# Softmax over rows of 32768: two column pieces of 8192 per tile, scaled by VectorE and ScalarE, with the small sums on GpSimd

## Chip, core, metric

One core of one Trainium2 chip. The metric is device time in microseconds of one execution. The span that a profile shows is about 2 us shorter than the time.

## The reference

```python
batch, seq, vocab = 16, 256, 32768          # float32 in, float32 out; temperature 1.0
scaled = logits / temperature
scaled = scaled - scaled.max(axis=-1, keepdims=True)
exp_scaled = np.exp(scaled)
return exp_scaled / exp_scaled.sum(axis=-1, keepdims=True)
```

These are 4096 rows. 536.87 MB must be read and as much written.

## The kernel before

A row is split in two halves, which lie in neighbouring partitions. A tile is 128 partitions x 16384 columns (64 rows, 8.39 MB), there are 64 tiles, and three buffers hold them in turn. Each full tile is loaded in two halves of 8192 columns. It is worked on in four pieces of 4096: VectorE takes the negated maximum of a piece, ScalarE does exp in place and sums. Then maxima and sums of the pieces and of the two half rows are combined by small instructions, and the pieces are scaled.

```python
_LOAD = (8192, 8192)
_PIECES = (4096, 4096, 4096, 4096)
_ON_DVE = (4096, 1024, 4096, 1024)      # columns of each piece scaled by VectorE, the rest by ScalarE
_HALF = 8192
...
for k in range(K):
    xc = xs[:, at[k] : at[k] + sizes[k]]
    nc.vector.tensor_reduce(out=nm[:, k : k + 1], in_=xc, axis=X, op=A.max, negate=True)
    ...
    nc.scalar.activation(out=xc, in_=xc, func=Exp, bias=nm[:, k : k + 1], scale=inv_t,
                         accum_out=ssum[:, k : k + 1])
nc.vector.tensor_reduce(out=nMh[:, 0:1], in_=nm, axis=X, op=A.min)
combine(nMh, A.min)                     # shuffle to the neighbour partition, then min
nc.scalar.activation(out=ee, in_=nm, func=Exp, bias=nMh[:, n_rounds : n_rounds + 1], scale=-1.0)
nc.vector.tensor_tensor_reduce(out=ttj, in0=ee, in1=ssum, ..., accum_out=Sh[:, 0:1])
combine(Sh, A.add)
nc.vector.reciprocal(out=rS, in_=Sh[:, n_rounds : n_rounds + 1])
nc.vector.tensor_scalar_mul(out=f, in0=ee, scalar1=rS)
for k in range(K):
    a, b, c = at[k], at[k] + on_dve[k], at[k] + sizes[k]
    if b > a:
        nc.vector.tensor_scalar_mul(out=xs[:, a:b], in0=xs[:, a:b], scalar1=f[:, k : k + 1])
    if c > b:
        nc.scalar.activation(out=xs[:, b:c], in_=xs[:, b:c], func=Copy, scale=f[:, k : k + 1])
    ...
    elif t and c % _HALF == 0:
        store(t, c - _HALF, c)          # issued from ScalarE's queue, the last two tiles' from SyncE
...
for t in range(G):
    normalise(t)
    if t and t + _BUFS - 1 < G:
        load(t + _BUFS - 1)             # issued from SyncE's queue
```

## Time and profile before

| | before |
|---|---|
| time, median (range) | 2493.26 us (2493.20 to 2493.26, 3 runs) |
| VectorE, ScalarE, GpSimd busy | 63%, 54%, 0% |
| DMA | 431 GB/s over the span |
| VectorE's instructions | 1217, 19 in a full tile |

The lines that carry the reading stand in the prediction below. In the DMA slices each digit is the busy share of a fortieth of the span in tenths. In a chain in order of time the columns are start, duration and what; in a group of instructions they are line, engine, operation, shapes, count, then busy us, mean ns, and idle us before with the engine that ended it. Two more lines of this kernel also belong here. The first is from the list of DMA queues (packets, MB, share of time), the second from the waits (us in total, times, longest):

```profile
q14 instruction: 22, 0.18, 0.0%
```

### The profile page before, as it was taken

What the parts mean: (1) busy time and instruction counts of PE and PEld (TensorE: products, weight loads), DVE (VectorE), ACT (ScalarE), POOL (GpSimd) and SP (SyncE); (2) the same over time, 40 slices, a digit from 0 to 9 for tenths busy, and PEclk for the clock granted to TensorE, in tenths of its full rate; (3) what the DMA queues carried; (4) which work ended last, traced back from release to release, by engine and by line L of the source; (5) the groups of instructions that cost most, each with busy time, mean ns of one, the idle gap of its engine ahead of it and who ended that gap; (6) DMA issues with size and microseconds to landing.
All of it is one profiled execution on the core that took longest, in us unless ns stands there. A gap on an engine that the chain in (4) does not pass through costs nothing.

```text
span 2491.5 us, 2807 instructions
## 1 busy us (share of the span) xinstructions
DVE 1580.1 (63%) x1217; ACT 1352.5 (54%) x711; POOL 0.2 (0%) x4
## 2 busy tenths in 40 slices
DVE  7765666655766657566675666756667566665654
ACT  6565555655556555555555554555545555465544
POOL 0000000000000000000000000000000000000000
DMA  9999999999999999999999999999999999999998
GB/s 412 436 430 436 431 435 431 433 433 430 437 430 437 430 436 430 437 429 436 431 436 431 434 432 432 434 431 436 430 437 429 437 430 436 430 437 430 436 431 370
DMA packets 38038, 1073.94 MB, mean 431 GB/s; under 512 B 4224, under 2 KB 4224, under 8 KB 4224
## 3 DMA queue, kind: packets, MB, share of 16 engines
q1 hardware_dynamic: 20160, 553.66, 51.6%
q10 hardware_dynamic: 17856, 520.10, 48.4%
q14 instruction: 22, 0.18, 0.0%
HBM read 536.87 MB, written 536.87 MB: 431 GB/s over the span
## 4 chain that ended last, share of the span: by engine, by line
DMA 68%; another core or an unknown queue 15%; DVE 11%; ACT 4%; issue 1%; SPq 0%; ACTq 0%
DMA out_dram<-x 41%; DMA x<-in_logits_dram 28%; DVE nm L108 8%; ACT x L115 3%; DVE x L148 3%; SPq L72 0%; DVE f L144 0%; ACT x L152 0%; ACT ee L129 0%; DVE rS L143 0%; DVE Sh L91 0%; DVE Sh L88 0%; DVE ttj L132 0%; ACTq L197 0%
## 5 line engine op out<-in xcount | busy, mean ns | idle before, releaser
L108 DVE TENSOR_REDUCE nm<-x 128x1 f32<-128x4096 f32 (+1 forms) x257 | 1119.1, 4395 | 639.0 <-DMA x<-in_logits_dram 639.0
L115 ACT ACTIVATE x<-x,nm 128x4096 f32<-128x4096 f32 (+1 forms) x257 | 949.3, 3694 | 976.4 <-DVE nm L108 976.0
L152 ACT ACTIVATE x<-x,f 128x3072 f32<-128x3072 f32 (+1 forms) x132 | 366.4, 2781 | 129.9 <-DVE f L144 73.5
L148 DVE TENSOR_SCALAR x<-x,f 128x1024 f32<-128x1024 f32 (+3 forms) x256 | 379.9, 1548 | 2.3
L132 DVE CUSTOM_DVE_ANT_0 ttj<-ee,ssum 128x4 f32<-128x4 f32 x64 | 10.4, 162 | 228.2 <-ACT ee L129 228.2
L115 ACT ACTIVATION_READ_ACCUMULATOR x<-x,nm 128x1 f32 x257 | 47.9, 186 | 0.0
L129 ACT ACTIVATE ee<-nm,nMh 128x4 f32<-128x4 f32 x64 | 18.0, 282 | 0.0
L144 DVE TENSOR_SCALAR f<-ee,rS 128x4 f32<-128x4 f32 x64 | 14.7, 229 | 2.2
L143 DVE RECIPROCAL rS<-Sh 128x1 f32<-128x1 f32 x64 | 10.5, 164 | 2.2
L91 DVE TENSOR_TENSOR Sh<-Sh 128x1 f32<-128x1 f32 x64 | 10.2, 159 | 2.2
L91 DVE TENSOR_TENSOR nMh<-nMh 128x1 f32<-128x1 f32 x64 | 10.2, 159 | 2.2
L127 DVE TENSOR_REDUCE nMh<-nm 128x1 f32<-128x4 f32 x64 | 10.0, 157 | 2.2
L88 DVE STREAM_SHUFFLE Sh<-Sh 128x1 f32<-128x1 f32 x64 | 9.7, 151 | 0.0
L88 DVE STREAM_SHUFFLE nMh<-nMh 128x1 f32<-128x1 f32 x64 | 9.7, 151 | 0.0
L115 ACT ACT_TABLE_LOAD x1 | 1.3, 1283 | 8.1 <-DMA x<-in_logits_dram 8.1
L132 DVE DVE_READ_ACCUMULATOR2_ANT Sh<- 128x1 f32 x64 | 5.2, 82 | 0.0
L88 DVE LOAD_MASK_SELECT nMh<-nMh x64 | 0.9, 14 | 2.8
L88 DVE LOAD_MASK_SELECT Sh<-Sh x64 | 0.9, 14 | 2.8
L183 POOL MEMSET const-bfloat16-1.0<- 128x1 bf16 x1 | 0.1, 101 | 0.0
L183 POOL MEMSET const-uint8-127<- 128x1 uint8 x1 | 0.1, 101 | 0.0
L183 POOL MEMSET const-float32-0.0<- 128x1 f32 x1 | 0.1, 98 | 0.2 <-issue 0.2
L183 POOL MEMSET const-float32-1.0<- 128x1 f32 x1 | 0.1, 98 | 0.0
## 6 DMA issues: line engine op xcount, KB each, us to landing
x<-in_logits_dram SPq DMA_DIRECT2D x124, 4096.0 KB, 31.3
out_dram<-x ACTq DMA_DIRECT2D x124, 4096.0 KB, 49.3
x<-in_logits_dram SPq DMA_DIRECT2D x7, 2048.0 KB, 20.6
out_dram<-x SPq DMA_DIRECT2D x2, 4096.0 KB, 33.5
out_dram<-x SPq DMA_DIRECT2D x3, 2048.0 KB, 17.3
x<-in_logits_dram SPq DMA_DIRECT2D x2, 1024.0 KB, 36.1
out_dram<-x SPq DMA_DIRECT2D x2, 1024.0 KB, 22.8
```

Of the source, the lines that this page charges most:

```text
L88: nc.vector.stream_shuffle(out=v[:, j + 1 : j + 2], in_=v[:, j : j + 1], mask=mask)
L91: nc.vector.tensor_tensor(out=v[:, j + 1 : j + 2], in0=v[:, j : j + 1], in1=v[:, j + 1 : j + 2], op=op,)
L108: nc.vector.tensor_reduce(out=nm[:, k : k + 1], in_=xc, axis=X, op=A.max, negate=True)
L115: nc.scalar.activation(out=xc, in_=xc, func=Exp, bias=nm[:, k : k + 1], scale=inv_t, accum_out=ssum[:, k : k + 1],)
L127: nc.vector.tensor_reduce(out=nMh[:, 0:1], in_=nm, axis=X, op=A.min)
L129: nc.scalar.activation(out=ee, in_=nm, func=Exp, bias=nMh[:, n_rounds : n_rounds + 1], scale=-1.0)
L132: nc.vector.tensor_tensor_reduce(out=ttj, in0=ee, in1=ssum, scale=1.0, scalar=0.0, op0=A.mult, op1=A.add, accum_out=Sh[:, 0:1],)
L143: nc.vector.reciprocal(out=rS, in_=Sh[:, n_rounds : n_rounds + 1])
L144: nc.vector.tensor_scalar_mul(out=f, in0=ee, scalar1=rS)
L148: nc.vector.tensor_scalar_mul(out=xs[:, a:b], in0=xs[:, a:b], scalar1=f[:, k : k + 1])
L152: nc.scalar.activation(out=xs[:, b:c], in_=xs[:, b:c], func=Copy, scale=f[:, k : k + 1])
L183: nc = _bacc.Bacc("TRN2", target_bir_lowering=False, num_devices=1)
```

## The change

The intent is fewer and larger instructions: two pieces of 8192, the first scaled by VectorE alone and the second by ScalarE alone, and the small sums off VectorE. The second tile keeps four pieces, so that the first tile's stores leave early; first and last tile are unchanged.

```diff
-_PIECES = (4096, 4096, 4096, 4096)
-_ON_DVE = (4096, 1024, 4096, 1024)
+_PIECES = (8192, 8192)
+_ON_DVE = (8192, 0)
+_SECOND_PIECES = (4096, 4096, 4096, 4096)
+_SECOND_ON_DVE = (4096, 4096, 2048, 0)
@@ combine takes the engine of its tensor_tensor
-    def combine(v, op) -> None:
+    def combine(v, op, engine=None) -> None:
+        engine = engine or nc.vector
...
+        if K == 2:
+            nc.gpsimd.tensor_tensor(out=ttj, in0=ee, in1=ssum, op=A.mult)
+            nc.gpsimd.tensor_tensor(
+                out=Sh[:, 0:1], in0=ttj[:, 0:1], in1=ttj[:, 1:2], op=A.add
+            )
+            combine(Sh, A.add, nc.gpsimd)
+            nc.vector.reciprocal(out=rS, in_=Sh[:, n_rounds : n_rounds + 1])
+            nc.gpsimd.tensor_scalar_mul(out=f, in0=ee, scalar1=rS)
+        else:
             ... (the sums on VectorE, as before)
@@ stores after all scaling
-            elif t and c % _HALF == 0:
-                store(t, c - _HALF, c)
+        for h in range(0, W if 0 < t < G - 1 else 0, _HALF):
+            store(t, h, h + _HALF)
```

More of the change, by code (lines that the diff above doesn't have):

```diff
@@ L48 @@
     n_rounds = _SPLIT.bit_length() - 1
-    K = max(len(_FIRST_PIECES), len(_PIECES), len(_LAST_PIECES))
+    K = max(
+        len(p) for p in (_FIRST_PIECES, _SECOND_PIECES, _PIECES, _LAST_PIECES)
+    )
     pool = ctx.enter_context(tc.tile_pool(name="fixed", bufs=1))
@@ L66, in cut @@
             return _LAST_PIECES, _LAST_ON_DVE, _LAST_PIECES
+        if t == 1:
+            return _SECOND_PIECES, _SECOND_ON_DVE, _LOAD
         return _PIECES, _ON_DVE, _LOAD
@@ L90, in combine @@
             )
-            nc.vector.tensor_tensor(
+            engine.tensor_tensor(
                 out=v[:, j + 1 : j + 2],
@@ L131, in normalise @@
         )
-        nc.vector.tensor_tensor_reduce(
-            out=ttj,
-            in0=ee,
-            in1=ssum,
-            scale=1.0,
-            scalar=0.0,
-            op0=A.mult,
-            op1=A.add,
-            accum_out=Sh[:, 0:1],
-        )
-        combine(Sh, A.add)
-        nc.vector.reciprocal(out=rS, in_=Sh[:, n_rounds : n_rounds + 1])
-        nc.vector.tensor_scalar_mul(out=f, in0=ee, scalar1=rS)
+        if K == 2:
+            nc.gpsimd.tensor_tensor(out=ttj, in0=ee, in1=ssum, op=A.mult)
+            nc.gpsimd.tensor_tensor(
+                out=Sh[:, 0:1], in0=ttj[:, 0:1], in1=ttj[:, 1:2], op=A.add
+            )
+            combine(Sh, A.add, nc.gpsimd)
+            nc.vector.reciprocal(out=rS, in_=Sh[:, n_rounds : n_rounds + 1])
+            nc.gpsimd.tensor_scalar_mul(out=f, in0=ee, scalar1=rS)
+        else:
+            nc.vector.tensor_tensor_reduce(
+                out=ttj,
+                in0=ee,
+                in1=ssum,
+                scale=1.0,
+                scalar=0.0,
+                op0=A.mult,
+                op1=A.add,
+                accum_out=Sh[:, 0:1],
+            )
+            combine(Sh, A.add)
+            nc.vector.reciprocal(out=rS, in_=Sh[:, n_rounds : n_rounds + 1])
+            nc.vector.tensor_scalar_mul(out=f, in0=ee, scalar1=rS)
         for k in range(K):
```

## The prediction

> **What bounds the kernel now.** I read the page from the top: busy shares, the slices of the span, the chain of waits; then the DMA queue's own waits, the issues, and one stretch in the middle in order of time.
>
> Busy shares and the DMA slices, from the page:
>
> ```profile
> DVE 1580.1 (63%) x1217; ACT 1352.5 (54%) x711; POOL 0.2 (0%) x4
> ...
> DMA  9999999999999999999999999999999999999998
> ...
> DMA packets 38038, 1073.94 MB, mean 431 GB/s; under 512 B 4224, under 2 KB 4224, under 8 KB 4224
> ```
>
> No compute engine is near full, while the DMA engines are at 90% or more in 39 of 40 slices and still moving in the last. The bytes are fixed: 536.87 MB in, 536.87 MB out.
>
> The chain of waits (page), and part of it in order of time:
>
> ```profile
> DMA 68%; another core or an unknown queue 15%; DVE 11%; ACT 4%; issue 1%; SPq 0%; ACTq 0%
> ```
>
> ```profile
> 1183.02 48.33 DMA out_dram<-x
> ...
> 1250.83 31.35 DMA x<-in_logits_dram
> ...
> 1282.20 8.76 DVE nm L108 x2
> ...
> 1299.15 48.32 DMA out_dram<-x
> ```
>
> The chain goes round one of three buffers: a store, a load, then compute. One turn is 1299.15 - 1183.02 = 116.13 us for three tiles, 38.71 us a tile. A tile moves 8.39 MB each way, so 16.78 MB / 38.71 us = 433.4 GB/s. The columns are start, duration and what; a transfer's duration includes waiting in its queue. That is the key to this page: 4.19 MB at 433.4 GB/s needs 9.68 us, yet a store is listed with 48. It stands behind other transfers.
>
> The timeline of that stretch (start, duration, engine, work):
>
> ```profile
> 1204.78 8.75 DVE L108 TENSOR_REDUCE nm<-x 128x1 f32<-128x4096 f32 x2 [10.26 <-DMA x<-in_logits_dram]
> ...
> 1217.27 0.28 ACT L129 ACTIVATE ee<-nm,nMh 128x4 f32<-128x4 f32 x1
> ...
> 1221.73 0.34 ACTq L81 DMA_DIRECT2D out_dram<-x  x1
> ...
> 1225.00 0.34 ACTq L81 DMA_DIRECT2D out_dram<-x  x1
> ...
> 1243.49 8.74 DVE L108 TENSOR_REDUCE nm<-x 128x1 f32<-128x4096 f32 x2 [10.26 <-DMA x<-in_logits_dram]
> ```
>
> Call T = 1204.76 the landing of a tile's second half. Its two stores are issued at T+17.0 and T+20.2. What still lies in the store queue then? The chain shows that the previous tile's first store, issued at 1183.02, lands at 1231.35, T+26.6; its second store lands one half-tile slot (38.71/2 = 19.36) later, T+45.9. So the store queue is not empty until T+45.9. The load queue has slack too: by the chain a store landed at 1231.35 and the next load went out at once, while the load ahead of it landed only at 1243.47, as the last row shows: 12 us of work was left. Hence the bound is DMA throughput; the tile's latency is hidden.
>
> **What the Trainium skill says.** "DMA: Bandwidth & Descriptors", section "Specifications", gives a fabric ceiling of 435 GB/s and an HBM limit near 358 GB/s per core. The trace agrees with the first (433.4) and goes past the second. At 435 GB/s the bytes alone take 2468 us, an estimate from that page; only 1% of the 2493 could go. The same page, section "Queues, rings and completion order", says each DMA engine goes round the queues that have work, packet by packet; so a later store costs nothing while both queues hold work. The trace agrees: a half-tile load takes a 19.36 us slot with stores beside it, twice 9.68. "GPSIMD Engine Reference", section "2.1 Instruction dispatch", describes software dispatch on eight cores and some 6 us for the first call of a freshly loaded routine. The trace of before has only four memsets of about 0.1 us on POOL and cannot confirm it.
>
> **The change part by part.** Durations by shape, from the groups by form:
>
> ```profile
> L108 DVE TENSOR_REDUCE nm<-x 128x1 f32<-128x4096 f32 x255 | 1114.7, 4412 | 639.0 <-DMA x<-in_logits_dram 639.0
> L115 ACT ACTIVATE x<-x,nm 128x4096 f32<-128x4096 f32 x255 | 945.3, 3707 | 976.4 <-DVE nm L108 976.0 <-ACT x L152 0.5
> L152 ACT ACTIVATE x<-x,f 128x3072 f32<-128x3072 f32 x124 | 354.0, 2856 | 127.6 <-DVE f L144 71.2 <-DVE x L148 34.1 <-DMA x<-in_logits_dram 22.4
> L148 DVE TENSOR_SCALAR x<-x,f 128x4096 f32<-128x4096 f32 x124 | 291.4, 2350 | 2.2
> L148 DVE TENSOR_SCALAR x<-x,f 128x1024 f32<-128x1024 f32 x124 | 92.7, 747 | 0.0
> ...
> L152 ACT ACTIVATE x<-x,f 128x1536 f32<-128x1536 f32 x7 | 10.5, 1564 | 2.3 <-DVE f L144 2.3
> ...
> L108 DVE TENSOR_REDUCE nm<-x 128x1 f32<-128x2048 f32 x2 | 4.5, 2275 | 0.0
> L115 ACT ACTIVATE x<-x,nm 128x2048 f32<-128x2048 f32 x2 | 4.0, 1986 | 0.0
> ```
>
> Two sizes of each operation give a line, and I extend it to 8192 columns. Reduce: 4412-2275 = 2137 ns per 2048, so 4412+2x2137 = 8.69 us. Exp: 1721 ns per 2048, 3707+2x1721 = 7.15 us. VectorE scale: (2350-747)/3072 = 0.522 ns a column, 2350+4096x0.522 = 4.49 us. ScalarE scale: (2856-1564)/1536 = 0.841, 2856+5120x0.841 = 7.16 us.
>
> VectorE, per full tile: reduces 4x4.41 to 2x8.69, -0.27; scaling 2x2.35+2x0.75 = 6.19 to 4.49, -1.70; the small product, its accumulator read, one add and f (0.162+0.082+0.159+0.229 on the page) go to GpSimd, -0.63. Sum -2.6; times the 61 tiles that take this path (all but the first, second and last of 64), about -159 us: busy 1580 to about 1421. ScalarE: exp 4x3.71 to 2x7.15, -0.53; two accumulator reads fewer at 0.186, -0.37; scaling 2x2.86 to 7.16, +1.45. Sum +0.55, +34 us: about 1386. GpSimd: four small operations a tile, 244 in all; I put each at 0.1 to 0.5 us, from memsets at 0.1 plus two inputs, an estimate. None of this busy time is on the bound.
>
> Latency after T: reduce 8.7, exp 7.15, ee 0.28 ends at about T+16.2 against T+12.8 before (T+3.4 later because the second exp starts after a whole half was reduced). Then the small sums: before from ee to f took about 1.1 us (ee ends 1217.55, scaling starts 1218.64). Now they cross VectorE and GpSimd five times; I take 2 us, at T+18.2. ScalarE's 7.16 ends at T+25.4. The rebuilt instruction order shows both store issues after that scaling, so they go out at T+25.4 and T+25.7, later by 8.4 and 5.5 us. The queue holds stores until T+45.9: 20 us to spare. So landings stay on their 19.36 us grid, the next loads go out at the same instants, and the next T is the same. What grows in compute shrinks as queueing: first-half stores show 48.3 - 8.4 = 40 us from issue to landing, second-half ones about 59. Sum on the path: 0.
>
> Ends: the first and last tile's code is unchanged. The second tile's first store is issued some 3 us later, behind the first tile's two stores. Near the end, the stores of tile 61 already wait for a load (the 22.4 us in the third row); the new order keeps such a wait, but now scaling comes before it. Tile 62 gives that back through larger pieces and should be stored within about 1 us of before, again with transfers queued ahead. I allow +-1 us.
>
> **The rivals.** (1) *Compute is on the chain, so its growth costs.* DVE 11% and ACT 4% stand in the chain, and 8.4 us times 61/3 turns would be +171 us: 2664. Against it: the queue wait in the same chain gives way first, 20 us worth. (2) *VectorE was the bound*, with 63% the busiest engine; -159 us would give 2334. Against it: VectorE waited 639 us for loads, and DMA is full. (3) *GpSimd is far slower than I think.* Small sums would have to take over 22 us a tile; each us beyond adds up to 61 us in all if the loads don't fill the gap. A first call of 6 us falls in the third tile alone and fits. (4) *Both stores issued together change the mixture on the DMA engines.* The four first quarter loads end at 4.9 us intervals, 2.10 MB each, 429 GB/s without stores: 1% below the mixed rate, so at most +20 us even if the mixture were lost, and it isn't, as both queues stay filled.
>
> **Range and chances.** The expected change is 0 with +-1 us from the ends and the odd hiccup, and three runs before agree within 0.1 us. I predict 2493.2 us, 2490.5 to 2496.5 in 8 of 10. Over 2% faster would need a DMA rate above 440 GB/s: 0.5%. Slower needs rival 1 or 3: 1.5%. Within 2%: 98%.
>
> **What would show it.** Right: DMA at 9s in every slice and near 431 GB/s; a turn of 116.1 us; loads' median still 31.3 us, stores' median fallen from 49.3 to between 40 and 59; VectorE near 1421, ScalarE near 1386. Wrong: slices of DMA under 9, a longer turn, a VectorE wait on GpSimd of many us, or first-half stores that take only about 20 us, which would mean the queue runs dry.

## More of the kernel before

```profile
DVE nm L108 <- DMA x<-in_logits_dram: 639.0, 73, 11.2
```

Queue 14 carries the engines' own instructions; 22 packets look like nothing. VectorE's wait of some 10 us per tile for a load is the slack of the computing engines.

## The result

| | before | after |
|---|---|---|
| median of 4 runs (range) | 2493.23 us (2493.11 to 2493.26) | 2490.66 us (2490.20 to 2491.36) |
| span of the profiled run | 2491.5 us | 2489.1 us |
| instructions in all; on VectorE | 2807; 1217 | 2138; 667 |

The ratio is 0.999, 95% interval 0.9973 to 1.0007. A ratio here is the mean time of one kernel's fast runs over that of the other's of the same rounds, so it is not quite the ratio of the medians. By that interval the two are the same; but the ranges don't touch, nor do they in any later comparison with the kernel before, so 2.6 us, a thousandth, is a difference worth explaining, if not worth having.

From the page of the changed kernel: busy times, the DMA slices, its packets, the instruction queue, the chain of waits, and the two largest groups of DMA issues.

```profile
DVE 1449.4 (58%) x667; ACT 1391.5 (56%) x406; POOL 53.5 (2%) x248
...
DMA  9999999999999999999999999999999999999999
...
DMA packets 38033, 1073.90 MB, mean 431 GB/s; under 512 B 4224, under 2 KB 4224, under 8 KB 4224
...
q14 instruction: 17, 0.14, 0.0%
...
DMA 62%; another core or an unknown queue 15%; DVE 13%; ACT 7%; POOL 1%; issue 1%; SPq 0%; ACTq 0%
...
x<-in_logits_dram SPq DMA_DIRECT2D x124, 4096.0 KB, 30.2
out_dram<-x ACTq DMA_DIRECT2D x124, 4096.0 KB, 45.2
```

The DMA engines are as full as before. The share of compute in the chain rose from 15% to 21% and nothing was lost by it. Part of the chain in order of time:

```profile
1186.99 44.36 DMA out_dram<-x
...
1250.75 30.05 DMA x<-in_logits_dram
...
1303.10 44.50 DMA out_dram<-x
```

A buffer's turn is 1303.10 - 1186.99 = 116.11 us, against 116.13 before. Inside it the store gave up 4 us, from 48.3 to 44.4. The timeline of the same stretch (start, duration, engine, work, idle time and who ended it):

```profile
1203.43 8.69 DVE L115 TENSOR_REDUCE nm<-x 128x1 f32<-128x8192 f32 x1 [7.88 <-DMA x<-in_logits_dram]
...
1219.27 0.28 ACT L136 ACTIVATE ee<-nm,nMh 128x2 f32<-128x2 f32 x1
...
1221.18 7.12 ACT L169 ACTIVATE x<-x,f 128x8192 f32<-128x8192 f32 x1 [1.64 <-POOL f L147]
1221.18 4.49 DVE L165 TENSOR_SCALAR x<-x,f 128x8192 f32<-128x8192 f32 x1 [0.42 <-POOL f L147]
1225.59 8.68 DVE L115 TENSOR_REDUCE nm<-x 128x1 f32<-128x8192 f32 x1
1225.71 2.97 ACTq L87 DMA_DIRECT2D out_dram<-x  x2
```

Three things are to be seen. The sums take 1221.18 - 1219.55 = 1.6 us. The first store goes out at 1225.71, when VectorE has scaled its half, while ScalarE is still busy with the other until 1228.30: its queue issues a DMA beside its own work. And VectorE still waits 7.88 us for the load in each tile; before it was 10.26.

**Where the 2.6 us are.** A transfer reports sixteen landings. The Trainium skill, "DMA: Bandwidth & Descriptors", section "Why a DMA increments its semaphore by 16 and not by 1", says that each of the DMA engines that share a transfer counts once when its part has landed; the trace agrees, with 16 landings for each. So their spread tells how far the DMA engines are apart. I worked the following out from the landings in the packed trace (first landing of the last store, and how much later the three slowest land, us):

```
kernel   first landing   lag of the three slowest    last landing
before        2483.09       4.33   6.22   7.56           2490.65
after         2482.39       4.76   5.54   5.85           2488.24
```

The first landing came 0.7 us earlier with the change, the last 2.4 us: most of the gain is a smaller lag of the slowest DMA engine, with which the kernel ends. Its lag grows in steps. In before, the loads land 19.36 us apart, but nine times the gap is over 19.9, mostly 20.3, and each time the slowest DMA engine falls back by another 1 us (20.33 - 19.36 = 0.97). Those long gaps are 253 or 272 us apart, 262 on average, and shortly before each of them stands a packet of 8192 bytes on queue 14: packets at 336, 602, 874, 1141 us, long gaps at 351, 603, 875, 1147. (The other packets on that queue come before no such gap.) In the changed kernel there are six, 427 or 466 us apart, 450 on average. 262 us is 6.8 tiles, or 6.8 x 19 = 129 VectorE instructions; 450 us is 11.6 tiles, or 11.6 x 10 = 116. So these packets look like blocks of VectorE's instructions, one per 116 to 129. The experiments test this.

### The profile page after: what moved, and what is told of

The parts are those of the page before. It is cut to its first block, busy times and chain, and to the rows that moved or that the text cites. A ratio compares the mean times of both kernels' runs of the same rounds, so it can differ in the third digit from the quotient of the medians.

```text
span 2489.1 us, 2138 instructions
## 1 busy us (share of the span) xinstructions
DVE 1449.4 (58%) x667; ACT 1391.5 (56%) x406; POOL 53.5 (2%) x248
## 4 chain that ended last, share of the span: by engine, by line
DMA 62%; another core or an unknown queue 15%; DVE 13%; ACT 7%; POOL 1%; issue 1%; SPq 0%; ACTq 0%
DMA out_dram<-x 36%; DMA x<-in_logits_dram 26%; DVE nm L115 9%; ACT x L122 6%; DVE x L165 4%; SPq L78 0%; POOL f L147 0%; ACT x L169 0%; ACT ee L136 0%; POOL ttj L141 0%; POOL Sh L98 0%; POOL Sh L142 0%; DVE Sh L95 0%; DVE rS L146 0%
## 5 line engine op out<-in xcount | busy, mean ns | idle before, releaser
L122 ACT ACTIVATE x<-x,nm 128x8192 f32<-128x8192 f32 (+1 forms) x135 | 913.5, 6767 | 961.2 <-DVE nm L115 945.4
L115 DVE TENSOR_REDUCE nm<-x 128x1 f32<-128x8192 f32 (+1 forms) x135 | 1112.0, 8240 | 497.2 <-DMA x<-in_logits_dram 497.2
L169 ACT ACTIVATE x<-x,f 128x8192 f32<-128x8192 f32 (+2 forms) x71 | 452.4, 6382 | 103.4 <-POOL f L147 99.9
L165 DVE TENSOR_SCALAR x<-x,f 128x8192 f32<-128x8192 f32 (+3 forms) x72 | 291.1, 4052 | 25.9 <-POOL f L147 25.8
L141 POOL TENSOR_TENSOR ttj<-ee,ssum 128x2 f32<-128x2 f32 x61 | 12.0, 196 | 2331.0 <-ACT ee L136 2331.0
L122 ACT ACTIVATION_READ_ACCUMULATOR x<-x,nm 128x1 f32 x135 | 25.2, 187 | 0.0
L147 POOL TENSOR_SCALAR f<-ee,rS 128x2 f32<-128x2 f32 x61 | 17.7, 290 | 18.1 <-DVE rS L146 18.1
L136 ACT ACTIVATE ee<-nm,nMh 128x2 f32<-128x2 f32 (+1 forms) x64 | 17.9, 280 | 0.0
L98 POOL TENSOR_TENSOR Sh<-Sh 128x1 f32<-128x1 f32 x61 | 11.9, 194 | 16.6 <-DVE Sh L95 16.6
L142 POOL TENSOR_TENSOR Sh<-ttj 128x1 f32<-128x1 f32 x61 | 11.8, 194 | 4.8
## 6 DMA issues: line engine op xcount, KB each, us to landing
x<-in_logits_dram SPq DMA_DIRECT2D x124, 4096.0 KB, 30.2
out_dram<-x ACTq DMA_DIRECT2D x124, 4096.0 KB, 45.2
```

The lines of the kernel that those rows point to most:

```text
L98: engine.tensor_tensor(out=v[:, j + 1 : j + 2], in0=v[:, j : j + 1], in1=v[:, j + 1 : j + 2], op=op,)
L141: nc.gpsimd.tensor_tensor(out=ttj, in0=ee, in1=ssum, op=A.mult)
L142: nc.gpsimd.tensor_tensor(out=Sh[:, 0:1], in0=ttj[:, 0:1], in1=ttj[:, 1:2], op=A.add)
L147: nc.gpsimd.tensor_scalar_mul(out=f, in0=ee, scalar1=rS)
```

## The experiments

Theory A: the kernel ends with the slowest DMA engine, and every block of VectorE's instructions that is fetched holds one DMA engine up by about 0.9 us; the change has fewer such blocks. Theory B: the time comes from the pieces and the moments at which stores go out. A second question is how much latency the kernel really hides. Each kernel gave correct results. Times are medians; the kernel before on the same chips had medians of 2493.12 to 2493.36.

### The pieces alone, and the sums alone

Pieces alone:

```diff
-        if K == 2:
+        if False:
```

> Only the pieces of the change (two of 8192, stores after the scaling); the small sums stay on VectorE. Theory A (the 2.5 us come from fewer instruction fetches: each fetched block of VectorE's instructions holds up one DMA engine by 0.9 us, and the slowest DMA engine ends the kernel): VectorE has 4 instructions more per full tile than the changed kernel, 244 in all, about 1.9 fetches, so 2490.7 + 1.7 = about 2492.3 us (2491.6 to 2493.0). Theory B (the gain comes from larger pieces and the later, closer stores): all of that is here, so 2490.7 us.

Sums alone, with four pieces, in tiles 2 to 62 (one more add, for four partial sums):

```diff
+        if 1 < t < G - 1:
+            nc.gpsimd.tensor_tensor(out=ttj, in0=ee, in1=ssum, op=A.mult)
+            nc.gpsimd.tensor_tensor(out=ttj[:, 0:2], in0=ttj[:, 0:2], in1=ttj[:, 2:4], op=A.add)
+            nc.gpsimd.tensor_tensor(out=Sh[:, 0:1], in0=ttj[:, 0:1], in1=ttj[:, 1:2], op=A.add)
+            combine(Sh, A.add, nc.gpsimd)
+            nc.vector.reciprocal(out=rS, in_=Sh[:, n_rounds : n_rounds + 1])
+            nc.gpsimd.tensor_scalar_mul(out=f, in0=ee, scalar1=rS)
```

> Only the sums on GpSimd, with the four pieces of before. Theory A: VectorE has 4 instructions fewer per full tile than before, 244 in all, 1.9 fetches fewer, so 2493.2 - 1.7 = about 2491.5 us (2491.0 to 2492.7). Theory B: pieces and stores are those of before, so 2493.2 us.

Measured: pieces alone 2491.41 us (2490.87 to 2492.44), sums alone 2492.10 us (2492.04 to 2492.87), before 2493.12. The parts give 1.7 and 1.0 us, which add up to about the whole's 2.6 (the runs of one kernel spread by up to 1.6 us, so this is no sharp test). That the sums alone gain speaks against B, as pieces and stores are those of before; the pieces alone came out a little better than A's range. The landings show why the sums alone gained less than A's 1.7 us. The DMA engine that falls back in steps, there every 310 us (8 tiles of 15 VectorE instructions), is 5.8 us late near the end instead of 7.6, as A has it. But another one falls back steadily, by some 0.05 us a load and without packets; it is 6.8 us late by then and is now the slowest. In before it is there too, 6.7 us late. What holds it up isn't shown.

### More tiny instructions on VectorE

After `combine(nMh, A.min)`, where VectorE waits 7.5 us for exp and the first sums anyway (n = 10 or 30):

```diff
+        if K == 2:
+            for i in range(n):
+                nc.vector.memset(junk[:, i : i + 1], 0.0)
```

> The changed kernel with 10 tiny VectorE memsets per full tile in time in which VectorE waits for the second exp (610 instructions, about 4.8 fetches). Theory A: 2490.7 + 4.8 x 0.9 = about 2495 us (2493.5 to 2496.5). Theory B: 2490.7 us, no change.

> As the last with 30 memsets per full tile (1830 instructions, about 14.3 fetches). Theory A: 2490.7 + 14.3 x 0.9 = about 2503.5 us (2500 to 2507). Theory B: no change, 2490.7 us; if only the fetched bytes counted, 117 kB at 433 GB/s would be 0.3 us.

Measured: 2494.36 us (2494.22 to 2494.46) with ten and 2510.53 us (2508.78 to 2513.02) with thirty. Ten are as A expected, and cost more than the whole change had gained. Thirty cost 19.9 us, more than A's range. The page of the run with thirty:

```profile
DVE 1473.9 (59%) x2497; ACT 1391.5 (56%) x406; POOL 53.5 (2%) x248
...
q14 instruction: 31, 0.25, 0.0%
```

VectorE is busy 24.5 us longer in all, in time in which it waits, yet the kernel ends 20 us later. Most long load gaps now come every 117 us, three tiles or 3 x 40 = 120 instructions. From the landings again:

```
kernel                first landing of the last store   slowest lag   long load gaps
changed kernel                  2482.39                    5.85             6
10 more on VectorE              2483.44                    8.00            10
30 more on VectorE              2498.47                    7.69            24
```

With ten it is mostly the lag of the slowest DMA engine that grows. With thirty, the other DMA engines lost 16 us too. By 1424 us the slowest lagged 10.4 us, near the 30.2 - 19.4 = 10.8 us of work that the load queue holds when the next load is issued; from then on the others fall back as well. They may run out of loads there, since the next load waits for the slowest. This fits the numbers but was not tested by itself. Thirty would be 14.3 more blocks at 0.97 us, 13.9 us. The profiled run, the fastest of the five, took 17.9 us more; a cluster of long gaps around 1500 us makes some 3 us of the rest, and its cause is open.

### The same number spread over three engines; all on GpSimd

Ten tiny instructions each on VectorE, ScalarE and GpSimd per full tile; then thirty on GpSimd:

```diff
+            if K == 2 and k == 1:               # ScalarE, before the second exp
+                for i in range(10):
+                    nc.scalar.activation(out=junka[:, i : i + 1], in_=nm[:, 0:1], func=Copy)
...
+            for i in range(10):
+                nc.vector.memset(junk[:, i : i + 1], 0.0)
+                nc.gpsimd.memset(junkp[:, i : i + 1], 0.0)
```

> The changed kernel with 30 tiny instructions more per full tile, 10 each on VectorE, ScalarE and GpSimd, where each engine waits anyway. Theory A with its detail (each engine's instruction blocks hold up a DMA engine of their own, so delays on different streams lie beside one another): VectorE's stream grows as in the run with 10 memsets, so about 2494.5 us (2493.5 to 2496.5). Rival detail (any block holds up the same engine, or what counts is the number of instructions in all): like the run with 30 on VectorE, about 2510 us. Theory B: 2490.7.

> The changed kernel with 30 tiny memsets more per full tile on GpSimd while it waits anyway (1830 instructions, about 14.3 blocks more). Theory A: GpSimd's stream holds up a DMA engine just as VectorE's does; its own lag is small at the start, so 2500 to 2511 us. If only VectorE's stream did it: 2490.7.

Measured: spread 2494.39 us (2494.15 to 2494.69), as with ten on VectorE alone and 16 us better than with thirty there. So the delays of the streams don't add up: A's detail, that each stream delays a DMA engine of its own, holds, though which of the sixteen carries which stream can't be read from this trace. Thirty on GpSimd: 2494.28 us (2494.24 to 2494.47). That missed: GpSimd's stream costs time too, 3.6 us, but far less than VectorE's 19.9 for as many instructions. The three runs with thirty more have 3968 instructions in all and 31 packets on queue 14 each, wherever the thirty are: one per 128 instructions (before has 22 for 2807, the changed kernel 17 for 2138).

The landings of the run on GpSimd show where the difference comes from. There are fifteen long gaps, of about 20.0 us, so a block costs some 0.65 us and not 0.97; and they fall on another DMA engine than VectorE's, which stands 5.9 us late near the end as in the changed kernel. The one with GpSimd's blocks gets to 9.2 us: 3.3 more than the slowest had, near the 3.6 measured, and still short of the 10.8 at which the others would be held up. So most of a longer stream's delay is hidden until its DMA engine is the slowest. Why a block of GpSimd's costs 0.65 us and not 0.97 is open. B expected no change from any added instruction and is out as the main cause.

### One and three long adds within the small sums

```diff
+            for _ in range(n):
+                nc.gpsimd.tensor_tensor(out=slow, in0=slow, in1=slow, op=A.add)   # 128x2048
             combine(Sh, A.add, nc.gpsimd)
```

> The changed kernel with one add over 128x2048 on GpSimd in the middle of the small sums of each full tile; I put it at about 4.5 us. In the changed kernel VectorE waits 7.9 us for the second half's load before it reduces it: its round of reduce, wait for exp, wait for sums, scale, reduce takes 38.7 - 7.9 = 30.8 us of each 38.7. With 4.5 more that is 35.3, below 38.7: no change, 2490 to 2492 us; VectorE's wait for the load falls to about 3.4 us. If compute on the chain of waits counted, 4.5 x 61/3 = +92 us: 2582.

> As the last with three such adds, about 13.5 us. As the prediction on record had it (20 us to spare until the store queue runs dry): no change, 2490 to 2492 us. By VectorE's own round: 30.8 + 13.5 = 44.3 us a tile instead of 38.7, so +5.6 x 61 = +340 us, about 2830 us, with DMA below 9 in most slices.

Measured: one add 2490.57 us (2490.53 to 2491.43), no change; three adds 2637.62 us (2637.49 and 2637.76), 147 us slower. With one add, the timeline and the groups of instructions:

```profile
1203.18 8.69 DVE L118 TENSOR_REDUCE nm<-x 128x1 f32<-128x8192 f32 x1 [4.64 <-DMA x<-in_logits_dram]
```

```profile
L149 POOL TENSOR_TENSOR slow<-slow 128x2048 f32<-128x2048 f32 x61 | 219.6, 3600 | 0.0
```

The add took 3.6 us, not the 4.5 that both expectations put (the figure of the page of the Trainium skill named at the end). 3.2 us of it came on top of the wait for the sums, the rest ran beside a shuffle, and VectorE's wait for the load fell by 3.2, from 7.9 to 4.6: the delay was paid out of this wait. With three, from the chain of waits and the groups on the page, and from the timeline:

```profile
DVE 52%; POOL 27%; ACT 18%; issue 1%; DMA 1%; another core or an unknown queue 0%; ACTq 0%; SPq 0%; POOLq 0%
...
L118 DVE TENSOR_REDUCE nm<-x 128x1 f32<-128x8192 f32 (+1 forms) x135 | 1106.1, 8234 | 12.2 <-DMA x<-in_logits_dram 12.2
```

```profile
1184.91 17.27 DVE L118 TENSOR_REDUCE nm<-x 128x1 f32<-128x8192 f32 x2
...
1226.24 17.27 DVE L118 TENSOR_REDUCE nm<-x 128x1 f32<-128x8192 f32 x2
```

The wait for loads is gone, DMA has left the chain, and a tile takes 1226.24 - 1184.91 = 41.33 us: VectorE's own round, 38.71 - 7.88 + 10.6 = 41.4 (10.6 is what the three adds put on top: ScalarE's wait for f rose from 1.6 to 12.2). That is 2.6 us over the 38.7 of DMA, times 61 tiles about 160; 147 were measured. The expectation of 2830 had put an add at 4.5 us; its mechanism was right. What falls is the claim that 20 us are to spare: 10.6 us were already too many. The DMA slices, by the way, still show 9s here in all but the last, at 407 GB/s: the digit doesn't tell a full DMA from one with a few per cent of gaps, the GB/s do.

### Two buffers instead of three

```diff
-_BUFS = 3
+_BUFS = 2
-_SETS = 3
+_SETS = 2
```

> The kernel before with two buffers instead of three. If time on the chain of waits is needed (rival 1 of the prediction: a buffer's turn takes 116 us), two tiles per 116 us give about 3700 us. If most of the turn is queueing: 20 us from landing to the second store, then store and load of a half at 9.7 to 19.4 us each make 40 to 59 us, less than the 77.4 us that DMA needs for two tiles, so DMA still bounds: 2490 to 2520 us, with stores' time from issue to landing fallen by some 38 us a turn together with the loads'.

> The changed kernel with two buffers. Hidden latency: 25 us to the second store, then as above 44 to 64 us, still under 77.4: 2490 to 2520 us, within 10 us of the other with two buffers. If two buffers expose the latency: slower than the other by up to 5 us x 31 = 155 us.

Measured: before with two buffers 2578.68 us (2574.48 to 2580.25), 3.4% over before; the changed kernel with two 2612.17 us (2601.60 to 2618.21). Both expectations were too low: the count assumed that DMA stays full, but it falls to 417 and 412 GB/s. It is far from the 3700 that a reading of the chain as needed time gives. And here the same change costs 33 us instead of gaining 2.6: this fits a longer latency that is no longer wholly hidden with a buffer less, and was not taken apart further.

### Two tries for a better version

One shuffle of both maxima and one reduce of four replace reduce, shuffle and min (9 VectorE instructions per full tile instead of 10; the first expectation miscounted 8). The first try also moved the second half's store to SyncE's queue; the second try left the stores alone.

```diff
+            nc.vector.stream_shuffle(
+                out=nm4[:, 2:4], in_=nm4[:, 0:2], mask=[i ^ 1 for i in range(32)]
+            )
+            nc.vector.tensor_reduce(
+                out=nMh[:, n_rounds : n_rounds + 1], in_=nm4[:, 0:4], axis=X, op=A.min
+            )
@@ first try only
-        engine = nc.sync if t >= G - 2 else nc.scalar
+        engine = nc.sync if t >= G - 2 or (t > 1 and a) else nc.scalar
```

> A try for a better version: the changed kernel with VectorE's instructions cut further (one shuffle of both maxima and one reduce of four in place of reduce, shuffle and min: 8 a tile instead of 10) and the second store of each full tile issued from SyncE instead of ScalarE, so that ScalarE's stream is shorter. Theory A: one fetch less on the longest streams, about 2489.7 us (2488.7 to 2490.7). Theory B: 2490.7; if stores behind loads in one queue hurt, slower by some us.

> The changed kernel with only VectorE's stream cut further (one shuffle of both maxima and one reduce of four; 9 instructions a full tile instead of 10, counting the mask loads), stores from ScalarE as in the changed kernel. Theory A: 61 instructions fewer are half a fetch, so 2490.0 to 2490.7 us, not to be told from the changed kernel. If the loss of the run with stores on SyncE came from this edit and not from the store queue: about 2524.

Measured: 2524.54 us (2521.05 to 2526.75) for the first, 2490.41 us (2490.03 to 2490.65) for the second, which can't be told from the changed kernel's 2490.66, as expected. So the store queue made the first slow. The DMA queue's own waits there:

```profile
SPq L87 <- ACT x L178: 2193.0, 62, 48.5
```

SyncE issues in order, and its next store waited 2193 us in all for ScalarE's scaling, with the loads of later tiles behind it; DMA fell to 426 GB/s. The chain of waits of that run shows it, the scaling, the store's issue and at once the load:

```profile
1206.23 7.13 ACT x L178
...
1213.38 0.34 SPq L87
...
1213.83 35.09 DMA x<-in_logits_dram
```

No version beat the changed kernel clearly.

## Why the prediction was right or wrong

The time (2490.66, predicted 2493.2, range 2490.5 to 2496.5) lay inside the range, near its lower edge, and "within 2%" held. That the lower edge held was partly luck: the prediction's one term for a change was +-1 us at the ends, what moved the time was not among its terms, and two of the four runs (2490.20 and 2490.47) lie below the range.

- **The bound is DMA throughput, latency is hidden.** Right: the same turn (116.1 us) and 431 GB/s; one add more of 3.6 us a tile changed nothing.
- **Durations of the large instructions.** Predicted for 8192 columns 8.69, 7.15, 4.49, 7.16 us; measured, in the groups by form of the changed kernel:

```profile
L115 DVE TENSOR_REDUCE nm<-x 128x1 f32<-128x8192 f32 x122 | 1059.3, 8683 | 481.1 <-DMA x<-in_logits_dram 481.1
L122 ACT ACTIVATE x<-x,nm 128x8192 f32<-128x8192 f32 x122 | 868.8, 7121 | 939.4 <-DVE nm L115 923.6 <-issue 15.8
L169 ACT ACTIVATE x<-x,f 128x8192 f32<-128x8192 f32 x61 | 434.5, 7122 | 99.9 <-POOL f L147 99.9
L165 DVE TENSOR_SCALAR x<-x,f 128x8192 f32<-128x8192 f32 x61 | 273.7, 4486 | 25.8 <-POOL f L147 25.8
```

- **Busy sums.** VectorE was predicted at 1421 and came to 1449.4 us, ScalarE at 1386 and 1391.5. The term that failed is the saving per tile: it added mean durations, but instructions back to back overlap on the page. The four scalings of before add up to 6.19 us and span 5.94 in its timeline, so joining them saved 1.45 us and not 1.70; likewise a pair of reduces spans 8.74 us and not 8.82.
- **GpSimd at 0.1 to 0.5 us each, the sums 2 us.** Right: 0.19 to 0.29 us each and 1.6 us.
- **"Both store issues after that scaling", at T+25.4 and T+25.7.** Wrong for the first: T+22.3, as VectorE ends (1225.71 against a landing at 1203.40). The second was at T+24.9. The order of instructions was read as if ScalarE's queue waited for its own arithmetic. So first stores show 44 us and not 40; the median of 45.2 lies within the 40 to 59 given. At the start, the second tile's first store went out 1.5 us later (65.24 against 63.70) and not 3.
- **"20 us to spare".** Wrong, and with it rival 3's "over 22 us a tile". It measured the store queue, and forgot that the next tile's work waits behind the sums on the same engines. The slack that binds stood in the timeline that the prediction quoted: `[10.26 <-DMA x<-in_logits_dram]`. The change lowered it to 7.9, and 10.6 us of delay broke it.
- **"Sum on the path: 0".** Near, but a term was missed: blocks of instructions hold up single DMA engines. The longest stream went from 1217 to 667 instructions and the slowest DMA engine's lag from 7.6 to 5.9 us; the rest of the 2.4 us between the two last landings is the 0.7 us by which the other DMA engines ended earlier, for which no cause is shown.
- **Rivals.** Compute in the chain (1) cost nothing with three buffers and some with two; relief of VectorE (2) brought no 159 us; the mixture on the DMA engines (4) kept its 431 GB/s (its "at most +20 us" should have been about 25: 1% of 2493).
- **"Loads' median still 31.3 us"** was 30.2; with one slow add it was 31.4 at the same time, so it means little.

## What to carry to other kernels

In a kernel bound by DMA, find the slack of the computing engines where they wait for loads each round (here 10.3 us of 38.7), and don't take a transfer's long time from issue to landing for it: both must hold, and the smaller one breaks first. Cutting or moving work then changes almost nothing, except that unrolled instruction streams are fetched by the same DMA engines: shorten the stream whose DMA engine lags most, or spread it over engines, and expect microseconds (2.6 of 2493 here). Don't put a store that waits for arithmetic ahead of loads on one issuing engine (34 us here).

## What the Trainium skill lacked or had wrong

- "Runtime: NRT & Kernel Launch", section "Instruction fetch mechanics", has instructions refilled in blocks of 16 KiB, "mostly hidden". These traces show packets of 8192 bytes, one per about 128 instructions (31 for 3968), and in a kernel bound by DMA they aren't hidden: some 0.97 us on one DMA engine per block of VectorE's and 0.65 per block of GpSimd's, 1830 extra memsets costing 19.9 us on VectorE, 3.6 us on GpSimd. No page that I found gives this price in the time of data transfers.
- "DMA: Bandwidth & Descriptors", section "Specifications": an HBM limit near 358 GB/s per core. One core alone held 433 GB/s, half reads and half writes, so the row by itself misleads for a core that runs alone. It is a share with two cores streaming, which the page says only further down. The fabric ceiling of 435 there agrees.
- "GPSIMD Engine Reference", section "3.1 Elementwise — side-by-side cycle accounting": 4497 ns for an fp32 add of 2048 columns. Here it took 3600 ns. Its section "2.1 Instruction dispatch" gives about 6 us for a first call of a freshly loaded routine; the first small product of the changed kernel took 0.20 us, 0.09 us after its input was ready, so no such cost shows; whether its routine was freshly loaded can't be seen.
- "DMA: Bandwidth & Descriptors", section "Issuing engines are not separate DMA queues", says that issuing from several engines only saves issue time. It lacks that a store which waits for compute holds back the loads issued after it on the same engine: one store per tile moved from ScalarE to SyncE cost 34 us.
